# Sliding-window gather: second halves of the split stores interleaved with whole stores, last two output slots stored by plain DMAs

## The chip, the cores and the metric

The kernel runs on one core of a Trainium2 chip. The metric is the device time of one execution in microseconds, as the median of several runs. Before the change it is 196.84 us, the median of 9 runs from 196.61 to 197.24.

## What is computed

The reference cuts overlapping 8x8 windows, four rows and four columns apart, out of every 64x64 image of a batch of 16 images with 64 channels, and lays each window out densely:

```
n_h = n_w = (64 - 8) // 4 + 1 = 15
for i in range(n_h):
    for j in range(n_w):
        result[:, i, j] = x[:, :, 4*i : 4*i + 8, 4*j : 4*j + 8]
```

The input is 16.78 MB of float32. Nearly every pixel is written four times, so the output (16, 15, 15, 64, 8, 8) has 58.98 MB. There is no arithmetic at all: the work is moving data.

## The kernel before

**Layout.** The 128 partitions hold 16 images x 2 channel halves x 4 row bands: partition p = 8*b + 4*ch + q has 32 channels of 16 image rows. The tile L holds the whole input this way. Sixteen plain DMAs of 1 MB (lines 49 to 54) load it: four chunks k of eight channels, four bands q each, with even bands issued on SP's queue and odd ones on ACT's.

**Windows.** One step of the kernel, `window(j, s, half)` (lines 87 to 119), makes the windows of output column j (0 to 14) and row slot s (0 to 3) for all images, channels and bands at once: band q and slot s give output row i = 4*q + s. VectorE (DVE) copies them out of L into the buffer G (line 101). For the last slot, s = 3, a window straddles two bands: line 103 copies its upper four rows, and line 104, a shuffle across partitions, fetches its lower four rows from the next partition. Band 3 has no output row for s = 3, so those windows are three quarters as many.

**Stores.** GpSimd (POOL) then issues one indirect DMA (line 109), which scatters the 128 partitions' pieces to output rows given by an index per partition (idx, or idx_last for s = 3, where band 3's rows are out of bounds and dropped). A whole store is 128 rows of 8 KB, 1 MB; with s = 3 it is 96 rows. A half store (half = 0 or 1) takes 16 of the 32 channels and moves rows of 4 KB, with the index tiles idx_h and idx_hlast.

**Buffer.** G has 18 units of half a window. A whole window takes two neighbouring units, a half one. The units go round: a copy must wait until the store that last used its unit has landed.

**Order.** The windows go column by column, four slots each, 60 in all. Lines 121 to 127 write the order out by hand. The first 12 windows (columns 0 to 2) are stored as halves: first all 12 first halves, which need only the load's chunks k = 0 and 1, then all 12 second halves, which need chunks 2 and 3. Then come the other 48 as whole windows. So POOL issues 72 stores; I number them 1 to 72 in this order. Stores 1 to 12 are the first halves, 13 to 24 the second halves, 25 to 72 whole windows.

**Semaphores.** The framework gives POOL's DMAs eight completion semaphores in turn. So each store n waits, at issue, for the landing of store n - 8: at most eight are out at a time. The plain DMAs of SP and ACT have eight more semaphores, in turn too.

Of the kernel before, what the change touches and what calls it, by code (L numbers as in the profile page):

```python
# [1 line left out]

# [4 lines left out]


@with_exitstack  # L10
def kernel(
    ctx: ExitStack,
    tc: tile.TileContext,
    x: bass.AP,
    window_size: int,
    stride: int,
    out: bass.AP,
):
    nc = tc.nc
    P = nc.NUM_PARTITIONS  # L20

    B, C, H, W = x.shape
    Bo, NH, NW, Co, WSo, WSo2 = out.shape
    WS = int(window_size)
    ST = int(stride)
    assert Bo == B and Co == C and WSo == WS and WSo2 == WS

    f32 = mybir.dt.float32
    i32 = mybir.dt.int32
    ALU = mybir.AluOpType  # L30
    HQ = 4
    CH = P // (B * HQ)
    CL = C // CH
    RB = H // HQ
    NSLOT = RB // ST
    NWIN = NH * NW
    CFREE = CL * WS * WS
    assert HQ == 4 and CH == 2 and WS == 2 * ST

    lpool = ctx.enter_context(tc.tile_pool(name="lpool", bufs=1))  # L40
    ipool = ctx.enter_context(tc.tile_pool(name="ipool", bufs=1))
    gpool = ctx.enter_context(tc.tile_pool(name="gpool", bufs=1))


    L = lpool.tile([P, CL, RB, W], f32)
    x_v = x.rearrange("b (ch cl) (hq r) w -> hq (b ch) cl (r w)", ch=CH, hq=HQ)
    NCH = 4
    cw = CL // NCH
    for k in range(NCH):
        for q in range(HQ):  # L50
            (nc.sync, nc.scalar)[q % 2].dma_start(
                out=L[q::HQ, k * cw : (k + 1) * cw, :, :],
                in_=x_v[q, :, k * cw : (k + 1) * cw, :],
            )


    def itile(name):
        return ipool.tile([P, 1], i32, name=name)

    pi, tb, tq, tc_, idx, idx_last = (itile(n) for n in ("pi", "tb", "tq", "tc", "idx", "idx_last"))  # L60
    nc.gpsimd.iota(pi[:, :], pattern=[[0, 1]], base=0, channel_multiplier=1)  # L61
    nc.vector.tensor_scalar(out=tb[:, :], in0=pi[:, :], scalar1=3, scalar2=None, op0=ALU.logical_shift_right)  # L62
    nc.vector.tensor_scalar(out=tc_[:, :], in0=pi[:, :], scalar1=2, scalar2=1, op0=ALU.logical_shift_right, op1=ALU.bitwise_and)  # L63
    nc.vector.tensor_scalar(out=tq[:, :], in0=pi[:, :], scalar1=HQ - 1, scalar2=None, op0=ALU.bitwise_and)  # L64
    nc.vector.tensor_scalar(out=tb[:, :], in0=tb[:, :], scalar1=float(NWIN * CH), scalar2=None, op0=ALU.mult)  # L65
    nc.vector.tensor_tensor(out=tb[:, :], in0=tb[:, :], in1=tc_[:, :], op=ALU.add)  # L66
    nc.vector.tensor_scalar(out=tc_[:, :], in0=tq[:, :], scalar1=float(NSLOT * NW * CH), scalar2=None, op0=ALU.mult)  # L67
    nc.vector.tensor_tensor(out=idx[:, :], in0=tb[:, :], in1=tc_[:, :], op=ALU.add)  # L68

    nc.vector.tensor_scalar(out=tq[:, :], in0=tq[:, :], scalar1=float(HQ - 1), scalar2=float(2 * B * NWIN * CH), op0=ALU.is_equal, op1=ALU.mult)  # L70
    nc.vector.tensor_tensor(out=idx_last[:, :], in0=idx[:, :], in1=tq[:, :], op=ALU.add)  # L71


    HCL = CL // 2
    idx_h, idx_hlast = itile("idx_h"), itile("idx_hlast")
    for d, e in ((idx_h, idx), (idx_hlast, idx_last)):
        nc.vector.tensor_scalar(out=d[:, :], in0=e[:, :], scalar1=2.0, scalar2=None, op0=ALU.mult)  # L77
    o_v = out.rearrange("b i j (ch cl) r w -> (b i j ch) (cl r w)", ch=CH)
    o_h = out.rearrange("b i j (ch cl) r w -> (b i j ch) (cl r w)", ch=2 * CH)
    nxt = [min(p + 1, 31) for p in range(32)]  # L80


    UNITS = 18
    G = gpool.tile([P, UNITS * HCL, WS, WS], f32, name="G")
    at = 0

    def window(j, s, half):
        nonlocal at
        cols = slice(j * ST, j * ST + WS)
        last = s == NSLOT - 1  # L90
        if half is None:
            n, c0 = 2, 0
            at += at % 2
        else:
            n, c0 = 1, half * HCL
        u = at % UNITS
        at += n
        cs = slice(c0, c0 + n * HCL)
        g = G[:, u * HCL : (u + n) * HCL, :, :]
        if not last:  # L100
            nc.vector.tensor_copy(out=g, in_=L[:, cs, s * ST : s * ST + WS, cols])  # L101
        else:
            nc.vector.tensor_copy(out=g[:, :, 0:ST, :], in_=L[:, cs, s * ST : RB, cols])  # L103
            nc.vector.stream_shuffle(out=g[:, :, ST:WS, :], in_=L[:, cs, 0:ST, cols], mask=nxt)  # L104
        if half is None:
            o, ix = o_v, (idx_last if last else idx)
        else:
            o, ix = o_h, (idx_hlast if last else idx_h)
        st = nc.gpsimd.indirect_dma_start(  # L109
            out=o,  # L110
            out_offset=bass.IndirectOffsetOnAxis(ap=ix[:, 0:1], axis=0),
            in_=g.rearrange("p c r w -> p (c r w)"),
            in_offset=None,
            element_offset=(s * NW + j) * CH * CFREE + (half or 0) * HCL * WS * WS,
            bounds_check=B * NWIN * CH * (1 if half is None else 2) - 1,
            oob_is_err=False,
        )
        tc.declare_no_dep(st.ins, group="stores", reason="each store writes rows of its own")
        tc.add_to_no_dep_group("stores", st.ins)

    order = [(j, s) for j in range(NW) for s in range(NSLOT)]
    EARLY = 12
    for half in range(2):
        for j, s in order[:EARLY]:
            window(j, s, half)
    for j, s in order[EARLY:]:
        window(j, s, None)


# [1 line left out]
_INS = ['x', 'window_size', 'stride']  # L131
_OUTS = [((16, 15, 15, 64, 8, 8), 'float32')]

_NUMBERS = {'window_size': 8, 'stride': 4}


# [26 lines left out]
```

## Time and profile before

| what | before |
| --- | --- |
| median of 9 runs | 196.84 us |
| the profiled execution's own time | 197.01 us |
| its span on the core | 195.1 us |
| DVE busy | 85.2 us, 44% of the span |
| POOL busy | 91.6 us, 47% of the span |
| moved by the DMA engines | 75.79 MB, mean 388 GB/s |
| of that, by POOL's stores (queue q0) | 10368 packets, 58.99 MB |
| read from HBM, written to HBM | 16.78 MB, 62.91 MB |

The span is what the profile's rows cover, and 1.9 us of the execution's time lie outside it. DVE and POOL are each busy for less than half of the span. The 16 DMA engines of the core are shared by three queues: q1 and q10 (the loads issued by SP and ACT) and q0 (the stores issued by POOL). Times in the text are microseconds from the start of the span.

### The profile page before, as it was taken

Reading aid. Unit: us, or ns where it says so; the run is one execution under the profiler, and the core shown is the slowest. Engines: PE = TensorE matmul, PEld = TensorE weight load, DVE = VectorE, ACT = ScalarE, POOL = GpSimd, SP = SyncE. Lnnn points to the kernel's source line nnn. Section 1 sums busy time; section 2 is a strip of 40 time slices with the busy share of each in tenths; the row PEclk is TensorE's granted clock in tenths of the full one; section 3 lists DMA queues with packets and bytes.
Section 4 is the critical chain, followed back from the end, with each engine's and each line's share of the span. In section 5 each row is a group of like instructions: output and inputs, shape, how many; then the busy total and the mean of one; then the engine's idle time right before and its main releaser. Section 6 shows DMA issues by size and latency. Waiting matters only on the chain.

```text
span 195.1 us, 458 instructions
## 1 busy us (share of the span) xinstructions
DVE 85.2 (44%) x119; POOL 91.6 (47%) x77
## 2 busy tenths in 40 slices
DVE  2000069100699745464647474747474746430000
POOL 0000047713478888888864545454545454530000
DMA  5999999999999879999999999999999999999970
GB/s 186 418 412 411 409 409 416 422 417 421 418 417 420 348 305 395 403 411 401 398 411 406 411 408 410 406 413 406 411 403 413 406 410 405 408 411 417 417 301 24
DMA packets 14723, 75.79 MB, mean 388 GB/s; under 512 B 1984, under 2 KB 1984, under 8 KB 8960
## 3 DMA queue, kind: packets, MB, share of 16 engines
q0 software_dynamic: 10368, 58.99, 74.7%
q1 hardware_dynamic: 2176, 8.39, 10.8%
q10 hardware_dynamic: 2176, 8.39, 10.6%
q14 instruction: 3, 0.02, 0.0%
HBM read 16.78 MB, written 62.91 MB: 408 GB/s over the span
## 4 chain that ended last, share of the span: by engine, by line
DMA 55%; issue 27%; POOL 7%; POOLq 1%; PEldq 0%
DMA out_dram<-G,idx_last 38%; DMA out_dram<-G,idx_hlast 10%; POOL out_dram L109 7%; DMA out_dram<-G,idx_h 7%; POOLq L158 1%; POOLq L109 0%; POOL pi L61 0%; PEldq L158 0%
## 5 line engine op out<-in xcount | busy, mean ns | idle before, releaser
L101 DVE COPY G<-L 128x2048 f32<-128x2048 f32 (+1 forms) x54 | 55.4, 1046 | 69.2 <-DMA L<-in_x_dram 39.2
L109 POOL DMA_INDIRECT out_dram<-G,idx x36 | 45.0, 1250 | 31.7 <-DMA out_dram<-G,idx 27.1
L109 POOL DMA_INDIRECT out_dram<-G,idx_h x18 | 22.9, 1275 | 37.6 <-DVE G L101 26.0
L109 POOL DMA_INDIRECT out_dram<-G,idx_last x12 | 16.9, 1410 | 8.9 <-DVE G L104 7.7
L104 DVE STREAM_SHUFFLE G<-L 128x1024 f32<-128x1024 f32 (+1 forms) x18 | 19.6, 1087 | 0.0
L103 DVE COPY G<-L 128x1024 f32<-128x1024 f32 (+1 forms) x18 | 11.6, 643 | 17.0 <-DMA out_dram<-G,idx 14.4
L109 POOL DMA_INDIRECT out_dram<-G,idx_hlast x6 | 6.4, 1075 | 3.7 <-DMA out_dram<-G,idx_hlast 2.2
L62 DVE TENSOR_SCALAR tb<-pi 128x1 int32<-128x1 int32 x1 | 0.2, 155 | 1.0 <-POOL pi L61 1.0
L61 POOL IOTA pi<- 128x1 int32 x1 | 0.1, 119 | 0.4 <-PEq L158 0.4
L104 DVE LOAD_MASK_SELECT G<-L x18 | 0.2, 12 | 0.0
L144 POOL MEMSET const-float32-0.0<- 128x1 f32 x1 | 0.1, 98 | 0.2 <-issue 0.2
L68 DVE CUSTOM_DVE_ANT_0 idx<-tb,tc 128x2 uint16<-128x2 uint16 x1 | 0.2, 160 | 0.0
L66 DVE CUSTOM_DVE_ANT_0 tb<-tb,tc 128x2 uint16<-128x2 uint16 x1 | 0.2, 159 | 0.0
L67 DVE TENSOR_SCALAR tc<-tq 128x1 int32<-128x1 int32 x1 | 0.2, 154 | 0.0
L77 DVE TENSOR_SCALAR idx_hlast<-idx_last 128x1 int32<-128x1 int32 x1 | 0.2, 154 | 0.0
L77 DVE TENSOR_SCALAR idx_h<-idx 128x1 int32<-128x1 int32 x1 | 0.2, 154 | 0.0
L71 DVE CUSTOM_DVE_ANT_0 idx_last<-idx,tq 128x2 uint16<-128x2 uint16 x1 | 0.2, 153 | 0.0
L65 DVE TENSOR_SCALAR tb<-tb 128x1 int32<-128x1 int32 x1 | 0.2, 152 | 0.0
L70 DVE TENSOR_SCALAR tq<-tq 128x1 int32<-128x1 int32 x1 | 0.1, 148 | 0.0
L64 DVE TENSOR_SCALAR tq<-pi 128x1 int32<-128x1 int32 x1 | 0.1, 145 | 0.0
L63 DVE TENSOR_SCALAR tc<-pi 128x1 int32<-128x1 int32 x1 | 0.1, 144 | 0.0
L144 POOL MEMSET const-uint8-127<- 128x1 uint8 x1 | 0.1, 118 | 0.0
(2 smaller groups left out, 0.2 us busy)
## 6 DMA issues: line engine op xcount, KB each, us to landing
L<-in_x_dram SPq DMA_DIRECT2D x8, 1024.0 KB, 19.8
L<-in_x_dram ACTq DMA_DIRECT2D x8, 1024.0 KB, 21.2
out_dram<-G,idx POOLq DMA_INDIRECT x36, 18.7
out_dram<-G,idx_h POOLq DMA_INDIRECT x18, 8.8
out_dram<-G,idx_last POOLq DMA_INDIRECT x12, 18.5
out_dram<-G,idx_hlast POOLq DMA_INDIRECT x6, 8.9
```

The costliest lines, as they stand in the source:

```text
L62: nc.vector.tensor_scalar(out=tb[:, :], in0=pi[:, :], scalar1=3, scalar2=None, op0=ALU.logical_shift_right)
L65: nc.vector.tensor_scalar(out=tb[:, :], in0=tb[:, :], scalar1=float(NWIN * CH), scalar2=None, op0=ALU.mult)
L66: nc.vector.tensor_tensor(out=tb[:, :], in0=tb[:, :], in1=tc_[:, :], op=ALU.add)
L67: nc.vector.tensor_scalar(out=tc_[:, :], in0=tq[:, :], scalar1=float(NSLOT * NW * CH), scalar2=None, op0=ALU.mult)
L68: nc.vector.tensor_tensor(out=idx[:, :], in0=tb[:, :], in1=tc_[:, :], op=ALU.add)
L71: nc.vector.tensor_tensor(out=idx_last[:, :], in0=idx[:, :], in1=tq[:, :], op=ALU.add)
L77: nc.vector.tensor_scalar(out=d[:, :], in0=e[:, :], scalar1=2.0, scalar2=None, op0=ALU.mult)
L101: nc.vector.tensor_copy(out=g, in_=L[:, cs, s * ST : s * ST + WS, cols])
L103: nc.vector.tensor_copy(out=g[:, :, 0:ST, :], in_=L[:, cs, s * ST : RB, cols])
L104: nc.vector.stream_shuffle(out=g[:, :, ST:WS, :], in_=L[:, cs, 0:ST, cols], mask=nxt)
L109: st = nc.gpsimd.indirect_dma_start(out=o, out_offset=bass.IndirectOffsetOnAxis(ap=ix[:, 0:1], axis=0), in_=g.rearrange("p c r w -> p (c r ...
L158: with _tile.TileContext(nc) as tc:
```

## The change

The change has two parts.

1. The order of the second halves. The 12 first halves stay at the head. After them, the second halves no longer come as one block of 12. They come in pairs, and after each pair follow two whole windows: second halves of windows 0 and 1, whole windows 12 and 13, second halves of 2 and 3, whole windows 14 and 15, and so on, until the 12 second halves are used up; the other whole windows follow as before.
2. The last two windows, (j, s) = (14, 2) and (14, 3), are no longer stored by POOL's indirect DMAs. Each is copied into G as before, and then stored by plain DMAs, one per band: four for slot 2, three for slot 3, with even bands on SP's queue and odd ones on ACT's. Each moves 32 partitions of 8 KB, 262 KB.

POOL issues 70 stores instead of 72; SP issues 12 DMAs instead of 8, ACT 11 instead of 8.

```diff
+    o_q = out.rearrange("b i j (ch cl) r w -> i j b ch (cl r w)", ch=CH)
+    order = [(j, s) for j in range(NW) for s in range(NSLOT)]
+    TAIL = 2
...
+    def free(st):
+        tc.declare_no_dep(st.ins, group="stores", reason="each store writes rows of its own")
+        tc.add_to_no_dep_group("stores", st.ins)
...
+        if (j, s) in order[len(order) - TAIL :]:
+            g_q = g.rearrange("(m q) c r w -> q m (c r w)", q=HQ)
+            for q in range(HQ - 1 if last else HQ):
+                free((nc.sync, nc.scalar)[q % 2].dma_start(out=o_q[q * NSLOT + s, j], in_=g_q[q]))
+            return
...
-        tc.declare_no_dep(st.ins, group="stores", reason="each store writes rows of its own")
-        tc.add_to_no_dep_group("stores", st.ins)
+        free(st)
 
-    order = [(j, s) for j in range(NW) for s in range(NSLOT)]
     EARLY = 12
-    for half in range(2):
-        for j, s in order[:EARLY]:
-            window(j, s, half)
-    for j, s in order[EARLY:]:
+    for j, s in order[:EARLY]:
+        window(j, s, 0)
+    for k, (j, s) in enumerate(order[EARLY:]):
+        if k < EARLY and k % 2 == 0:
+            window(*order[k], 1)
+            window(*order[k + 1], 1)
         window(j, s, None)
```

## The prediction, made before the changed kernel ran

> **What bounds the kernel now.** I begin with the page's slices, because nothing is computed here: either the DMA engines are full or something starves them.
>
> ```profile
> DMA  5999999999999879999999999999999999999970
> GB/s 186 418 412 411 409 409 416 422 417 421 418 417 420 348 305 395 403 411 401 398 411 406 411 408 410 406 413 406 411 403 413 406 410 405 408 411 417 417 301 24
> ```
>
> A slice is 4.88 us. The 16 DMA engines are full from the second slice on at 400 to 420 GB/s, whatever DVE (44%) and POOL (47%) do. The time is bytes over rate, plus the slices that fall short: the first (load start), slices 14 and 15 (63 to 73 us), and the end. The table of stretches around them:
>
> ```profile
> 60.00:64.00 4.00, 4.00 (x6) 3.33 (x3) 1.00 1.03 419
> 64.00:66.00 2.00, 1.81 (x3) 1.76 (x1) 1.00 1.03 420
> 66.00:68.00 2.00, 1.08 (x2) 1.69 (x2) 1.00 0.63 252
> 68.00:70.00 2.00, 0.97 (x1) 1.70 (x2) 1.00 0.58 234
> 70.00:72.00 2.00, 0.41 (x1) 1.39 (x3) 1.00 0.91 367
> 72.00:74.00 2.00, 1.48 (x3) 1.70 (x2) 1.00 0.84 328
> ...
> 173.00:184.00 11.00, 0.00 (x0) 0.96 (x1) 1.00 1.01 416
> ...
> 186.00:188.00 2.00, 0.00 (x0) 0.00 (x0) 1.00 0.87 361
> 188.00:191.00 3.00, 0.00 (x0) 0.00 (x0) 1.00 0.47 197
> 191.00:195.00 4.00, 0.00 (x0) 0.00 (x0) 1.00 0.00 0
> ```
>
> Columns are the stretch, its length, DVE busy, POOL busy, clock, DMA share and GB/s. Two holes are to be seen: 66 to 74, and 186 to the end. Why the first exists is in POOL's timeline (start, duration, idle before and what ended it):
>
> ```profile
> 57.21 1.01 POOL L109 DMA_INDIRECT out_dram<-G,idx_h  x1 [0.30 <-DMA out_dram<-G,idx_h]
> 58.53 1.81 POOL L109 DMA_INDIRECT out_dram<-G,idx_h  x1 [0.30 <-DMA out_dram<-G,idx_hlast]
> 60.65 1.97 POOL L109 DMA_INDIRECT out_dram<-G,idx_h  x1 [0.30 <-issue]
> 62.92 1.01 POOL L109 DMA_INDIRECT out_dram<-G,idx_hlast  x1 [0.30 <-issue]
> 64.24 2.70 POOL L109 DMA_INDIRECT out_dram<-G,idx_h  x1 [0.30 <-issue]
> 67.25 1.84 POOL L109 DMA_INDIRECT out_dram<-G,idx_h  x1 [0.31 <-issue]
> 69.39 0.96 POOL L109 DMA_INDIRECT out_dram<-G,idx_h  x1 [0.30 <-DMA out_dram<-G,idx_h]
> ```
>
> POOL never idles more than 0.3 us, yet needs 10.86 us for the five issues from 58.53 to 69.39, 2.17 each. A half store is only 0.52 MB, 1.26 us of DMA at 413 GB/s. POOL feeds slower than the engines eat; store 20 has landed on every engine at 67.7 (landing records), and store 21 was handed over only at 66.94. An issue alone takes 0.96 + 0.30 = 1.26; the long ones lie beside DVE's 2048-element copies, which run ahead for the whole windows.
>
> **Part 1, the order.** Removed and added: nothing. POOL's and DVE's lists hold the same half stores and copies; only their order from store 13 on changes. Moved: from 13 to 36 the mix is half, half, whole, whole.
>
> *The need of DMA per issue.* A whole store of the steady stage costs 2.53 us (the early half of the engines lands eight stores, six full and two of three quarters, every 18.94 us: 18.94/7.5), a half 1.26, last-slot ones 1.9 and 0.95. Eight stores of the mix (3 halves, 1 last half, 3 wholes, 1 last whole) need 3.78 + 0.95 + 7.58 + 1.9 = 14.2 us, 1.775 each instead of about 1.2.
>
> *The supply by POOL.* Copies per eight stores, from the groups by shape: 3 x 0.688 + 0.542 + 3 x 1.225 + 0.694 = 7.0 us. In the worst stretch (58.53 to 69.39) 7.83 us of copies lay beside POOL and stretched 5 x 1.26 = 6.3 to 10.86: 58% of copy time is lost to POOL. So eight issues take 8 x 1.26 + 0.58 x 7.0 = 14.1 us, 1.77 each. Measured means agree: 1.72 over 51.27 to 71.92, 1.67 over the whole stores from 71.92 to 100.23. Supply matches need, and the backlog covers what is left: at 51.27, when store 13 is issued, first halves keep the engines until 58.4, when store 12 lands. Store 36 is the tightest: 24 stores need 3 x 14.2 = 42.6, so store 35 lands at 58.4 + 42.6 - 1.9 = 99.1. Store 36 must be handed over about 1.0 us earlier (a store that found the engines idle landed 2.3 us after its issue ended, 1.26 of it moving) with 1.3 for its issue, so start by 96.8: 45.5 us for 23 intervals, **1.98 each**. POOL at 1.67 to 1.8 is inside.
>
> *The Trainium skill speaks against this.* Its page "SBUF — State Buffer", section "The 'DVE blocks DMA' trap (SWDGE)", has such copies shut POOL out of a shared port completely while they run. Taken at its word, with POOL always ready, eight issues take 10.1 + 7.0 = 17.1 us, 2.14 each, and (2.14 - 1.98) x 23 = 3.7 us would be lost, more than the present hole. The rows have a stall but only 58% of it.
>
> *Other cover.* DVE needs 7.0 + 2.0 of shuffles per 14.2 us; G's 18 units are 22 us of DMA work, and eight stores of the mix are 12 units, so unit waits bind no earlier than now.
>
> *The gain.* Lost in 66 to 74 by share against 1.01: 2 x (0.38 + 0.43 + 0.10 + 0.17) = 2.2. By landings on the later engines: store 20 at 67.7 to 25 at 77.1 is 9.4, against 3 x 1.26 + 0.95 + 2.53 = 7.26: 2.1. On the earlier engines it is 66.9 to 76.7, 2.5. The later decide the end: **-2.1**, bounds 0 and -2.5. What is late next is DMA itself.
>
> **Part 2, the tail.** Removed: POOL's last two issues (0.96 each, hidden: the engines have some 18 us of work left when POOL ends). Added: 4 + 3 plain DMAs, as many bytes and rows per engine. Rows: loads issue in 0.6 to 0.9 us each on SP and ACT, which idle there; their first packets came 0.8 (SP) and 3.2 us (ACT) after the first issue ended.
>
> *A wait is added.* In the changed kernel's instruction list the last window's first copy waits not only for its unit but for four semaphores of the plain queues: those of window (14,2)'s four DMAs. Behind it on DVE stand only its shuffle, and for that wait its three DMAs and the final waits of SP. Its length: window (14,2)'s copy ended at 169.2, now 167.1. How plain and indirect DMAs share engines the trace shows: between 32 and 45 us, with all three queues loaded, q0, q1 and q10 started 416, 467 and 449 packets, a third each. So 32 KB per engine and plain queue, beside as much of q0, take 96 KB / 26 GB/s = 3.7 us, and with issue and first packet (1.4, then 0.8 to 3.2) they land at 173 to 175.5. Copy and shuffle 1.9, then the same again: the last plain store lands by 179 to 184. POOL's stores still have work until about 189. Nothing is exposed: **0**. If plain DMAs waited behind all that q0 holds (18.76 us, the last-slot store in the chain), the copy would come at 186, the last three DMAs could start only at 188 to 191 and the engines would stand idle: +0 to +2.5.
>
> *The end.* Sixteen landings of the last store fall in two groups, 187.8 to 188.1 and 191.2 to 191.4: half the engines are 3.3 us late, the 0.47 above. They fall back only while DVE and POOL work (19.5 us per eight stores against 18.9; in the last interval 18.9 both). Rows per engine don't change, so this stays: 0 (bounds -1.6, were it evened out, and +0.4, if the earlier drained hole had hidden some of it). After the last landing SP needs 0.6 us for its waits, but POOL's closing drain, begun at 173.00, ends only at 194.35, 3.0 after that landing, and the end follows in 0.7. POOL's last store still lands last if thirds hold, so the drain stays too: 0. If q0 finished 2.4 us or more before the plain DMAs, the drain would lie under them: -2.4.
>
> *A second rule.* "DMA: Bandwidth & Descriptors", section "Rules for kernel authors", wants at least 1 MiB per DMA, and its fit of 2.0 us plus bytes at 436 GB/s makes seven of 262 KB cost an estimated 18 us in a row. No row here has so small a plain DMA; queued 1 MB loads ran at 410 to 420 GB/s with such costs hidden.
>
> **The sum.** Profiled execution 197.01 = span 195.1 + 1.9. Order -2.1, tail 0, end 0: span 193.0, time 194.9. The profiled run lies 0.17 above the median of 196.84, so the median forecast is **194.7**, own range 194.2 to 195.3.
>
> **Rivals.**
> - *The hole is only partly closed* (12%): POOL's interval passes 1.98 for a stretch, as 2.17 did for five issues; half to three quarters is lost again, 195.3 to 196.4. For: the 2.70 issue. Against: the means 1.72 and 1.67.
> - *POOL becomes the bound of the whole mixed stage* (7%, slower): DVE has more to copy per issue than in the second-half block now, over 24 issues instead of 12. At 2.17 each, (2.17 - 1.98) x 23 = 4.4 is lost against 2.1 now: 199.1. It decides from 1.98 on, and is slower than before from 1.98 + 2.1/23 = 2.07.
> - *Plain stores end the kernel* (8%): q0 served first, as priced, up to +2.5 on 194.7, so 195.5 to 197.2; evenly in the three signs. Against: the thirds.
> - *POOL's drain is hidden* (11%): q0 finishes early because plain packets get less than a third, but still in time: 192.3 to 194.2. Against: the thirds, again.
> - Forecast 62%.
>
> The changed order and queues are in the instruction lists, so that the change isn't done at all is excluded.
>
> Faster by over 0.2% (what a measurement of this kernel can tell): 0.62 + 0.11 + 0.11 + 0.03 = 0.87; within: 0.04; slower: 0.09. The range leaves out the upper end of the second rival and the tips of the others: 192.8 to 196.5.
>
> **What will show it.** Right: no stretch between 60 and 110 under 0.95 DMA share, POOL's mean interval from store 13 to 36 below 1.98; the last window's copy at 173 to 177, plain DMAs landed before 185; last landing near 189.2, span 193.0. Wrong: a hole that has moved to 75 to 100 us; a copy of the last window after 184; a drain of POOL that ends within 1 us of the last landing.

## The result and the profile after

The changed kernel takes 197.96 us (median of 10 runs, 197.62 to 198.68) against 196.81 us in the runs beside it: a ratio of 1.0061, 95% interval 1.0053 to 1.007. It is slower by 0.6%, where 194.7 was forecast with a range up to 196.5. The profiled span is 195.7 us against 195.1.

The page's slices again, now of the changed kernel:

```profile
DMA  5999999999999999999999999999999999999940
GB/s 181 419 411 413 409 410 415 421 418 421 418 419 430 424 415 435 415 401 411 407 407 409 402 419 402 419 404 414 405 410 407 407 410 410 409 303 407 397 156 7
```

The two slices that stood at 348 and 305 GB/s are gone: 424 and 415 now. A new low of 303 stands in slice 36 (171 to 176 us), and its DMA digit is still 9. The table of stretches of the changed kernel (stretch, length, DVE busy, POOL busy, clock, DMA share, GB/s), first around the old hole, then around the tail:

```profile
64.00:66.00 2.00, 0.96 (x1) 1.77 (x1) 1.00 0.98 403
66.00:68.00 2.00, 1.97 (x4) 1.59 (x2) 1.00 1.06 436
68.00:70.00 2.00, 1.10 (x2) 1.70 (x2) 1.00 0.99 418
70.00:72.00 2.00, 1.23 (x1) 1.70 (x2) 1.00 0.99 410
72.00:74.00 2.00, 1.55 (x2) 1.70 (x2) 1.00 1.06 436
```

```profile
170.00:171.00 1.00, 0.00 (x0) 0.00 (x0) 1.00 1.02 426
171.00:174.00 3.00, 0.00 (x0) 0.00 (x0) 1.00 1.04 292
174.00:177.00 3.00, 0.00 (x0) 0.00 (x0) 1.00 0.98 339
177.00:180.00 3.00, 0.98 (x3) 0.00 (x0) 1.00 1.02 421
184.00:186.00 2.00, 0.00 (x0) 0.00 (x0) 1.00 0.94 365
186.00:188.00 2.00, 0.00 (x0) 0.00 (x0) 1.00 0.53 156
188.00:190.00 2.00, 0.00 (x0) 0.00 (x0) 1.00 0.45 164
190.00:192.00 2.00, 0.00 (x0) 0.00 (x0) 1.00 0.16 66
```

The first hole is closed: nothing under 0.98 between 64 and 74. In the second table compare the last two columns. Before, share and rate fell together: engines without work. From 171 to 177 the share is 1.0 and the rate 292 to 339: all engines have work, and packets take longer on average. The trace's records of single packets say the same. In those 6 us POOL's packets of 8 KB took 405 ns on average, those of SP's queue 475 and of ACT's 378, against 322 from 150 to 165 us. It is not every packet that is slow: 63% took the usual 320 ns or less, while 36% took over 340 and the longest 1404. From 150 to 165 us 8% took over 340 and the longest 554.

The timeline of DVE, POOL and the plain issues shows what hung on that:

```profile
165.37 1.23 DVE L108 COPY G<-L 128x2048 f32<-128x2048 f32 x1 [1.22 <-DMA out_dram<-G,idx]
166.05 1.39 POOL L121 DMA_INDIRECT out_dram<-G,idx  x1 [1.06 <-DMA out_dram<-G,idx]
166.63 16.27 SPq L115 DMA_DIRECT2D out_dram<-G  x4
166.63 14.87 ACTq L115 DMA_DIRECT2D out_dram<-G  x3
179.02 0.69 DVE L110 COPY G<-L 128x1024 f32<-128x1024 f32 x1 [12.43 <-DMA out_dram<-G]
```

The copy of window (14, 2) starts at 165.37 instead of 168.01: by then the order has gained 2.6 us. The plain DMAs of that window are issued from 166.63, their first packets start at 171.3 and 172.6, and the last lands at 178.8. So the last window's copy waits 12.43 us and starts at 179.02, and its own plain DMAs run from 183.4. A landing is the moment when one of the 16 engines reports its share of a DMA as done. POOL's last store lands on the first half of the engines by 184.7 and on the other half at 190.0 to 192.0, and the last plain store at 191.0. In the kernel before, the last landing was at 191.4.

### The profile page after: what moved, and what is told of

The parts are those of the page before. It is cut to its first block, busy times and chain, and to the rows that moved or that the text cites. A ratio compares the mean times of both kernels' runs of the same rounds, so it can differ in the third digit from the quotient of the medians.

```text
span 195.7 us, 467 instructions
## 1 busy us (share of the span) xinstructions
DVE 85.1 (43%) x119; POOL 90.3 (46%) x75
## 4 chain that ended last, share of the span: by engine, by line
DMA 65%; issue 22%; POOL 3%; DVE 2%; ACTq 0%; POOLq 0%; DVEq 0%; PEldq 0%
DMA out_dram<-G,idx 33%; DMA out_dram<-G,idx_hlast 18%; DMA out_dram<-G,idx_h 8%; DMA out_dram<-G 6%; POOL out_dram L121 3%; DVE G L111 1%; DVE G L108 1%; DVE G L110 0%; ACTq L115 0%; POOLq L121 0%; POOL pi L61 0%; DVEq L110 0%; DVEq L108 0%; PEldq L170 0%
## 5 line engine op out<-in xcount | busy, mean ns | idle before, releaser
L121 POOL DMA_INDIRECT out_dram<-G,idx_h x18 | 21.8, 1210 | 37.7 <-DVE G L108 26.2
L121 POOL DMA_INDIRECT out_dram<-G,idx_last x11 | 16.3, 1484 | 7.5 <-DVE G L111 5.2
L121 POOL DMA_INDIRECT out_dram<-G,idx_hlast x6 | 7.1, 1190 | 3.7 <-DMA out_dram<-G,idx_hlast 2.2
```

The costliest lines, as they stand in the source:

```text
L121: st = nc.gpsimd.indirect_dma_start(out=o, out_offset=bass.IndirectOffsetOnAxis(ap=ix[:, 0:1], axis=0), in_=g.rearrange("p c r w -> p (c r ...
```

## The experiments

All ratios are against the kernel before, run beside each. The first four take the change apart: theory A, the plain stores are slow and slow the stores beside them; theory B, the wait of the last copy for the plain stores is what costs; rival C, the order gives its gain back. Most of the slow kernels came out up to 0.7 us above the range that was expected of them (tail_one, copies_first, contig_source, spare_same, spare_pad); the theories lie further apart than that.

**order_only.** All stores leave by POOL, in the new order.

```diff
-    TAIL = 2
+    TAIL = 0
```

> Only the new order of the second halves; all 72 stores leave by POOL. Theory A (the plain stores are slow packets and slow the indirect stores beside them; the order gained what was forecast): 194.3 to 194.8, with no stretch under 0.95 DMA share before 184 and the end as before, half of the engines 3.3 us later than the others. Theory B (the wait of the last window's copy for the plain stores makes the loss; the order gained): the same 194.3 to 194.8. Rival C (the order gives back later what it gains at 66 to 74, by slower whole stores): 196.5 to 198.0.

Measured: 194.65 us, ratio 0.988 (0.9862 to 0.9898), span 192.4. Its stretches:

```profile
66.00:68.00 2.00, 2.00 (x4) 1.65 (x2) 1.00 1.05 432
68.00:70.00 2.00, 1.04 (x2) 1.69 (x2) 1.00 1.02 430
...
182.00:184.00 2.00, 0.00 (x0) 0.00 (x0) 1.00 1.03 426
184.00:186.00 2.00, 0.00 (x0) 0.00 (x0) 1.00 0.50 209
186.00:188.00 2.00, 0.00 (x0) 0.00 (x0) 1.00 0.48 201
```

No low rate until half of the engines finish at 184.6; the other half finishes at 188.7, 2.7 earlier than before. Rival C falls. Part 1 alone is the forecast, 194.7, almost to the digit, and with some luck: the kernel before took 197.05 beside it instead of 196.84, and the gain was 2.4 instead of 2.1.

**tail_only.** The old order, with the plain stores.

```diff
-    for j, s in order[:EARLY]:
-        window(j, s, 0)
...
+    for half in range(2):
+        for j, s in order[:EARLY]:
+            window(j, s, half)
+    for j, s in order[EARLY:]:
```

> Only the plain stores of the last two windows, in the old order. Theories A and B: the loss of the tail stands by itself, some 3 us, so 199.4 to 200.6, with the hole at 66 to 74 still there. Rival C (the tail costs nothing, the order is at fault): 196.5 to 197.2.

Measured: 200.64 us, ratio 1.018 (1.0153 to 1.0206). The tail alone costs 1.8%, some 3.6 us, and 1.0061/0.988 = 1.018 is its price in the changed kernel too: the parts add.

**tail_one.** New order; only the last window leaves by plain DMAs, so that no copy waits for one.

```diff
-    TAIL = 2
+    TAIL = 1
```

> New order; only the last window, three plain DMAs of 262 KB, leaves by SP and ACT, so no copy waits for a plain store any more. Theory A: cost by bytes, 3/7 of some 3 us: 195.3 to 196.0, and packets above 340 ns while they are in flight. Theory B: no cost, 194.3 to 194.8, packets at 310 to 325 ns.

Measured: 196.65 us, ratio 0.9976 (0.9964 to 0.9989): 2.0 above order_only for 0.79 MB, more than its share by bytes (3/7 of 3.6 is 1.5) and above the 195.3 to 196.0 of theory A. From 175 to 179 the rate was 291 GB/s, POOL's packets at 351 ns, the plain ones at 423 and 614. The cost needs no wait, as A says; its size is not simply by bytes.

**copies_first.** New order, all seven plain DMAs, issued only after both last copies.

```diff
-                free((nc.sync, nc.scalar)[q % 2].dma_start(out=o_q[q * NSLOT + s, j], in_=g_q[q]))
+                later.append(((nc.sync, nc.scalar)[q % 2], o_q[q * NSLOT + s, j], g_q[q]))
...
+    for eng, to, of in later:
+        free(eng.dma_start(out=to, in_=of))
```

> New order and all seven plain DMAs, but they are issued only after both last copies, so that the copy of the last window doesn't wait for them. Theory A: the slow packets stay, 196.8 to 198.0. Theory B: the wait was the loss, 194.3 to 195.0.

Measured: 198.43 us, ratio 1.0066 (1.005 to 1.0082), the same as the whole change. The last copy starts at 168.01 instead of 179.02, and nothing is won. Theory B falls.

**What makes the packets slow?** The next four start from copies_first: S, the source with every fourth partition; D, the destination; Q, the plain queues beside POOL's.

**contig_source.**

```diff
-            g_q = g.rearrange("(m q) c r w -> q m (c r w)", q=HQ)
+            g_q = g.rearrange("(q m) c r w -> q m (c r w)", q=HQ)
```

> As copies_first, but plain DMA q reads 32 neighbouring partitions (32q to 32q+31) in place of every fourth one; destinations, sizes and queues stay, so the rows of the last two windows hold the wrong data. Theory S (the strided source makes the packets slow): 194.3 to 195.3, plain packets at 310 to 330 ns. Theory D (the scattered destination, two 8 KB rows per image, all 16 images at once) and theory Q (the plain queues beside POOL's queue, whatever they move): 197.8 to 198.8, packets of 350 to 700 ns.

Measured: 199.09 us, ratio 1.0121 (1.0104 to 1.0138), 296 GB/s from 171 to 182. Neighbouring partitions are no cure; it is a little slower. S falls in this form. The run differs from copies_first in one more thing: its first plain DMAs were issued at 166.78, before the last copy, instead of 169.93.

**scratch_dest.**

```diff
+    spare = nc.dram_tensor("spare", (2, P, CFREE), f32).ap().rearrange("t (b ch q) f -> t q b ch f", b=B, ch=CH)
...
-                later.append(((nc.sync, nc.scalar)[q % 2], o_q[q * NSLOT + s, j], g_q[q]))
+                later.append(((nc.sync, nc.scalar)[q % 2], spare[s - 2, q], g_q[q]))
```

> As copies_first, but the plain DMAs write to a spare dense HBM tensor, rows 32 KB apart, so the last two windows of the output stay unwritten. Source, sizes and queues stay. Theory D: 194.3 to 195.3, packets at 310 to 330 ns. Theories S and Q: 197.8 to 198.8.

Measured: 194.44 us, ratio 0.9875 (0.9859 to 0.9892), as fast as order_only. The same bytes, source and queues, and all three queues' packets at 314 to 315 ns, none above 329 from 174 to 184 us, where copies_first has 35% above 340. Stretches of copies_first, and then of scratch_dest, while the plain stores run:

```profile
174.00:176.00 2.00, 0.00 (x0) 0.00 (x0) 1.00 1.08 283
176.00:178.00 2.00, 0.00 (x0) 0.00 (x0) 1.00 0.97 311
178.00:180.00 2.00, 0.00 (x0) 0.00 (x0) 1.00 1.00 336
```

```profile
174.00:176.00 2.00, 0.00 (x0) 0.00 (x0) 1.00 1.02 422
176.00:178.00 2.00, 0.00 (x0) 0.00 (x0) 1.00 0.97 401
178.00:180.00 2.00, 0.00 (x0) 0.00 (x0) 1.00 1.04 430
```

So plain stores beside POOL's cost nothing as such, and something about their destination does. I read this as "the addresses", which turned out to be wrong.

**pool_plain.** The same plain DMAs on POOL's queue.

```diff
-                later.append(((nc.sync, nc.scalar)[q % 2], o_q[q * NSLOT + s, j], g_q[q]))
+                later.append((nc.gpsimd, o_q[q * NSLOT + s, j], g_q[q]))
```

> As copies_first, but the same seven plain DMAs are issued by POOL on its own queue. Theory Q: 194.3 to 195.5, packets at 310 to 330 ns, all in queue q0. Theories S and D: 197.5 to 198.8, slow packets also in q0.

Measured: 197.01 us, ratio 0.9997 (0.9977 to 1.0016), between the two expectations. The last landing is at 190.7, 2.0 later than in order_only, so these DMAs cost time in q0 too, and q0 has slow packets now: a mean of 412 ns from 179 to 180 us and 436 from 184 to 185. But POOL also waits 1.4 to 2.1 us before five of the seven issues, and from 180 to 182 the share falls to 0.87; the two costs were not parted here. Q falls as the whole cause.

**plain_eight.** The last eight windows by plain DMAs.

```diff
-    TAIL = 2
+    TAIL = 8
```

> As copies_first with the last eight windows stored by plain DMAs, issued after the last copy. Theory Q: once POOL's queue has run dry, the plain stores run alone at 400 to 420 GB/s with packets at 310 to 330 ns. Theories S and D: they stay at 280 to 350 GB/s when alone, with packets of 350 ns and more. The total is above copies_first in both cases, since the engines idle until the last copy: 200 to 208.

Measured: 197.38 us, ratio 1.0032 (1.0018 to 1.0047), below the 200 to 208 expected. Stretches while the plain stores run alone:

```profile
172.00:182.00 10.00, 0.00 (x0) 0.00 (x0) 1.00 1.01 359
182.00:192.00 10.00, 0.00 (x0) 0.00 (x0) 1.00 0.98 349
```

Alone they reach 354 GB/s at a full share: slow by themselves, with POOL's queue empty. That the total is low all the same has part of its reason at the end: the last plain store lands at 194.3 and the span ends 1.0 later, where the span of the kernel before ends 3.8 after its last landing. POOL's closing drain had long been done (171.9).

**Which property of the destination?** First the addresses: P, their pattern; N, the neighbourhood of POOL's stores.

**spare_same and spare_pad.** The scratch tensor gets the output's layout, and then one window more per image.

```diff
+    spare = nc.dram_tensor("spare", (B, NH * NW, C, WS, WS), f32).ap().rearrange("b (i j) (ch cl) r w -> i j b ch (cl r w)", i=NH, ch=CH)
...
+                later.append(((nc.sync, nc.scalar)[q % 2], spare[q * NSLOT + s, j], g_q[q]))
```

```diff
+    spare = nc.dram_tensor("spare", (B, NWIN + 1, C, WS, WS), f32).ap().rearrange("b n (ch cl) r w -> n b ch (cl r w)", ch=CH)
...
+                later.append(((nc.sync, nc.scalar)[q % 2], spare[(q * NSLOT + s) * NW + j], g_q[q]))
```

> As scratch_dest, but the spare HBM tensor has the size and layout of the output, so the plain DMAs write with the output's own strides (3.69 MB from image to image) at another base; the last two windows of the output stay unwritten. Theory P (the pattern of the addresses, one row of every image at once, is slow wherever it lies): 197.8 to 198.8, packets of 350 to 700 ns. Theory N (it is slow because POOL's stores write neighbouring rows of the same tensor at that time): 194.3 to 195.3, packets at 310 to 330 ns.

> As spare_same, with one window (16 KB) more per image in the spare tensor, so that the images lie 3.70 MB apart. Theory P in the form that the exact stride makes the rows collide: 194.3 to 195.5. In the form that any such wide spread is slow: 197.5 to 198.8. Theory N: 194.3 to 195.3 here too.

Measured: 199.06 us (ratio 1.0111, 1.0092 to 1.0129) and 199.18 us (1.0117, 1.0099 to 1.0136). N falls, and so does an exact collision of the stride.

**spread_4mb and spread_16mb.** As spare_pad with 15 and 60 windows per image.

```diff
-    spare = nc.dram_tensor("spare", (B, NWIN + 1, C, WS, WS), f32)
+    spare = nc.dram_tensor("spare", (B, 15, C, WS, WS), f32)
...
-                later.append(((nc.sync, nc.scalar)[q % 2], spare[(q * NSLOT + s) * NW + j], g_q[q]))
+                later.append(((nc.sync, nc.scalar)[q % 2], spare[q * NSLOT + s - 2], g_q[q]))
```

> As spare_same, but the spare tensor has 15 windows per image, so the 16 images lie 246 KB apart and span 3.9 MB; the last two windows of the output stay unwritten. If the distance decides gradually: 194.4 to 196.5, packets between those of scratch_dest (313 to 317 ns) and spare_same (310 to 1200 ns). If only the order of the rows within an engine (two rows next to each other) decides: 198.5 to 199.3 like spare_same.

> The same with 60 windows per image: 983 KB apart, 15.7 MB in all. Distance gradually: 195.5 to 198.5, above spread_4mb. A threshold below 1 MB, or the order of rows: 198.5 to 199.3. A threshold above 1 MB: 194.3 to 195.0.

Measured: 199.53 us (ratio 1.0144, 1.0093 to 1.0195) and 198.76 us (1.0105, 1.007 to 1.0139). Each has two runs only, but all lie above 198.2: from 246 KB to 3.7 MB no distance of the images takes the loss away.

**one_queue.** copies_first with all plain DMAs on SP.

```diff
-                later.append(((nc.sync, nc.scalar)[q % 2], o_q[q * NSLOT + s, j], g_q[q]))
+                later.append((nc.sync, o_q[q * NSLOT + s, j], g_q[q]))
```

> As copies_first, with all seven plain DMAs on SP's queue. If two plain queues at once are needed for the loss: 194.5 to 196. If the addresses alone do it, in any queue: 197.0 to 199.

Measured: 198.36 us, ratio 1.0095 (1.0073 to 1.0117). One plain queue is enough for the loss.

**rows_apart and rows_next.** The trace labels the plain DMAs of every slow kernel with a destination of 2 x 16 elements of 8 KB (two channel halves, 16 images), and those of scratch_dest with 32 x 1: there the rows are 32 equal steps apart and the two loops, images and channel halves, fold into one. These two kernels test the form against the place; each differs from scratch_dest in one line.

```diff
+    spare = nc.dram_tensor("spare", (2, B, 9, CFREE), f32).ap()[:, :, 0:8, :].rearrange("t b (ch q) f -> t q b ch f", ch=CH)
```

```diff
+    spare = nc.dram_tensor("spare", (2, P, CFREE), f32).ap().rearrange("t (q b ch) f -> t q b ch f", b=B, ch=CH)
```

> As scratch_dest, but the images lie 72 KB apart instead of 64 KB, so that the rows, still 32 KB apart within an image, can no longer be described as 32 equal steps and become 16 x 2 as in the changed kernel; the last two windows of the output stay unwritten. Theory F (the 16 x 2 form of the destination is slow, wherever it lies): 198.0 to 199.5. Theory R (two rows next to each other are slow): 194.2 to 195.0.

> As scratch_dest, but the 32 rows of a plain DMA lie next to each other, 8 KB apart, still described as 32 equal steps. Theory F: 194.2 to 195.0. Theory R: 198.0 to 199.5.

Measured: rows_apart 199.0 us (ratio 1.0111, 1.007 to 1.0152), rows_next 194.42 us (0.9879, 0.9863 to 0.9896). First rows_apart, then rows_next:

```profile
174.00:176.00 2.00, 0.00 (x0) 0.00 (x0) 1.00 1.11 266
176.00:178.00 2.00, 0.00 (x0) 0.00 (x0) 1.00 0.93 291
```

```profile
174.00:176.00 2.00, 0.00 (x0) 0.00 (x0) 1.00 1.01 418
176.00:178.00 2.00, 0.00 (x0) 0.00 (x0) 1.00 1.01 418
```

Eight kilobytes more between the images, which keep the two loops from folding, take the rate from 417 to 292 GB/s from 174 to 184 us. Theory R falls: rows next to each other are fast. Theory F fits every run: on the plain queues, stores of the two-loop form are slow and those of one loop fast, at whatever distance and in whichever tensor. One thing goes along with the form and isn't parted from it: the two fast destinations have an image pitch (the distance from one image's rows to the next's) of 64 and 16 KB, powers of two, and no slow one has such a pitch. One loop of equal steps at another pitch, say rows 12 KB apart, was not run. That POOL's stores write rows at the output's own pitch at 409 GB/s (100 to 150 us in the kernel before) speaks against the pitch, but POOL's are another kind of DMA.

**A version that beats both.** late_three, late_two and late_one take the new order and only the last window plain, but make its copy reuse units that POOL frees late, so that the plain DMAs come when q0 is nearly or wholly empty. At the end the last landing on q0 is followed by POOL's drain of 3.0 us, which plain stores can cover.

```diff
-        u = at % UNITS
+        u = (at - 6 if (j, s) == order[-1] else at) % UNITS
```

(8 in late_three, 6 in late_two, 4 in late_one; TAIL is 1.)

> New order; only the last window leaves by three plain DMAs, and its copy takes the units of the store three windows before it (13,3), so that it waits for that landing (about 179.5) and the plain DMAs come when POOL's queue is nearly empty. If POOL's closing drain runs 3.0 us from the last landing of POOL's own stores and not of all stores, it now lies under the plain stores: 193.2 to 194.2, with the last plain landing some 1.3 us before the end. If the drain waits for all DMAs, or the slow packets still meet POOL's stores: 195.0 to 196.6.

> As late_three, with the units of the store two windows before the last of POOL's (14,0), which lands at about 182: the plain DMAs come after POOL's queue is empty on all engines. Drain under the plain stores: 193.0 to 194.0. Drain after all: 195.5 to 197.

> As late_two, with the units of POOL's last store but one (14,1), which lands at 184.4: the plain DMAs start at about 187.5, when POOL's last store has landed everywhere, and end at about 190. POOL's drain, 3.0 after 186.8, is over by 189.8, so the end is the last plain landing plus 1.3: 193.3 to 194.2, no more than 0.5 below late_two.

Measured: late_three 195.32 us (ratio 0.992, 0.9907 to 0.9934), late_two 194.08 us (0.9862, 0.9846 to 0.9877), late_one 194.05 us (0.9863, 0.9846 to 0.9879). In late_three the plain stores still met POOL's, as its second expectation has it; in late_two they met the late half too (first plain packet at 185.2, POOL's last landing at 188.0), though it was expected to be empty. In these two, late_two and late_one, POOL's drain ends 2.95 us after the last landing of POOL's own stores (at 190.95 and 189.93), while plain stores landed until 190.0 and 190.8: it follows its own queue alone. Both beat the kernel before by 1.4% and the changed one. Their intervals overlap with that of order_only, so whether they beat it isn't settled. late_one gained nothing on late_two: its drain was over earlier, but its last plain store landed later.

## Why the prediction was wrong, step by step

- **The bound and the first hole: right.** DMA was starved from 66 to 74 by POOL's pace, and the order closes the hole. Its gain was put at 2.1, from the later half of the engines; order_only gained 2.4 in the medians (197.05 to 194.65) and 2.7 in the spans, a little beyond the bound of 2.5.
- **POOL's pace: right.** 1.77 per issue was worked out, with a limit of 1.98. In the changed kernel stores 13 to 36 start from 51.45 to 90.79: 39.34/23 = 1.71. The Trainium skill's page "SBUF — State Buffer", section "SBUF: two separate sides" (its note on the 'DVE blocks DMA' trap), has DVE's copies shut POOL out while they run. Taken at its word, an estimated 2.14 per issue and 3.7 us lost, it is not borne out: share and rate show no hole between 64 and 110.
- **The step that failed: the tail's term, "96 KB / 26 GB/s = 3.7 us ... Nothing is exposed: 0".** The thirds hold roughly (from 173 to 176 q0, SP's and ACT's queues started 48, 34 and 42 packets). The 26 GB/s per engine do not: from the first plain packet to the last landing it took 7.5 us (171.3 to 178.8), not 3.7. They came from packets of other DMAs, POOL's stores and the loads, and were put on a form of DMA that the trace did not hold. With plain stores in flight the sixteen engines moved 315 GB/s from 171 to 177, not 410, and again too little from 186 on (156 GB/s at a share of 0.53, where order_only has 201 at 0.48). The term was 0; it measured +3.6 (tail_only, 1.018). That the plain DMAs are small, 262 KB, is not the reason: in scratch_dest the same seven cost nothing.
- **The added wait: wrong in length, and not the cost.** It was put at landings from 173 to 175.5 and was 178.8, since the first packets came 4.1 (SP) and 5.4 us (ACT) after the first issue ended, not 0.8 and 3.2, and the packets were slow. But copies_first, without the wait, takes as long.
- **The rival "Plain stores end the kernel"** named the right place, the tail, with the wrong mechanism (q0 served first) and too small a price (+0 to +2.5). The last landing was still POOL's, 192.0 against 191.0 for the plain stores. The bounds of the unknown cost missed: a plain store was bounded by its waiting, never by its own rate, and never by what it does to the packets beside it.
- **The end: right in kind.** The drain follows the last landing of POOL's stores by 2.9 (192.0 to 194.9). Half of the engines stay late, in order_only by 4.0 instead of 3.3: 0.7 more, in the direction that the bound of +0.4 was kept for. That the hole had let them catch up fits this, but isn't shown.

What stays open is why the two-loop form is slow, or what goes along with it. The trace doesn't tell which engine moved which row. The Trainium skill's page "DMA: Bandwidth & Descriptors", section "Why a DMA increments its semaphore by 16 and not by 1", lets the number of engines depend on the slowest dimension of the two access patterns, and has the counts of unused engines written at once, without waiting for data. Here all sixteen landings of a plain DMA come one after another while its data move (173.6 to 175.0 for the first), so too few engines is not the reason. That contig_source, another source under the same form, ran at 296 GB/s instead of 312 may point to how rows and engines are paired, or only to its earlier start; that is a guess. Plain stores cut once more, by channel half, would have one loop and the real destination; that was not tried.

## What to carry to other kernels

Before stores are moved to another queue, look for a row of that very form in the trace: direction, loops of the destination, size. If there is none, its own rate is an unknown with a price, and so is the rate of what runs beside it. When a stretch is slow, read the DMA share and the GB/s together: a low share is missing work, a full share with a low rate is slow packets, though not all of them need be slow. Where two edits come as one change, price and test them apart: here -2.4 and +3.6 us.

## What the hardware showed unexpectedly

- Plain DMAs of 32 rows of 8 KB beside POOL's indirect stores: 417 GB/s in all when the destination's rows are one loop of equal steps (scratch_dest, rows_next). When they are two loops (2 x 16), 291 (tail_one) to 315 GB/s (spare_pad) on two plain queues and 337 on one (one_queue); 354 GB/s with these DMAs alone (plain_eight). In these stretches most packets take the usual 309 to 320 ns, and between 29% (plain_eight) and 45% (tail_one) of them more than 340.
- POOL's closing drain ends 2.7 to 3.2 us after the last landing of POOL's own DMAs (169.2 to 171.9 in plain_eight, 188.7 to 191.7 in order_only, 190.7 to 193.9 in pool_plain), whatever other queues still do.
- Eight of the sixteen engines fall some 3% behind while whole stores leave beside DVE's and POOL's work (19.5 against 18.9 us per eight stores in the kernel before) and not when these rest. Its cause was not looked into.
